# E of the first pair behind the split of x's weighted copy on ACT instead of behind weight splits

## The chip, the core and the metric

The kernel runs on one core of a Trainium2 chip. The core has a matrix engine (PE, with its weight loads PEld), a vector engine (DVE), an activation engine (ACT), a third elementwise engine that here mostly issues DMAs (POOL), and a sequencer for DMA issues (SP). Each engine runs its own instructions in order and waits on semaphores for the others. The metric is the device time of one execution in microseconds.

## The reference: what is computed

One layer of a hybrid encoder, for 256 frames of a new stream and 16 frames of each of 8 running streams, so 384 rows of width 2048, all in float32:

```
u = RMSNorm(x); P = u @ w_in          # columns: pool | z | x,B,C | dt | gates
branch A: trailing-window means of pool columns, per-group linear map, scale
branch B: causal conv (4 taps) + SiLU on x,B,C; Mamba-2 scan over chunks:
  cum   = cumsum(dt * A)
  decay = exp(where(causal, cum[t] - cum[s], -inf))
  y     = einsum(cb[..., None] * decay, x * dt) + C.h * exp(cum)
  h     = h * exp(last) + einsum(B, exp(last - cum), x * dt)
  y += D * x;  RMSNorm(y * SiLU(z))
m = sigmoid(gA) * (A @ w_pool_proj) + sigmoid(gB) * (B @ w_ssd_proj)
x += RMSNorm(m @ w_out);  x += RMSNorm(relu(RMSNorm(x) @ w_up)^2 @ w_down)
```

There are 64 heads of 64 channels in 8 groups with a state of 128. `cb * decay`, for two heads at a time, is what the kernel calls E.

## The kernel before

**Matmuls in three parts.** Every weight block (128 x 1024 float32, 512 KB, eight 128 x 128 tiles) is loaded by SP into a tile `w` and then split in two: ACT makes the rounded high part `wh` (L70) and DVE the rest, `wl = w - wh` (L71). A product is three matmuls per tile: `wh` times the high part of x (L98), `wh` times its low part (L99), `wl` times its high part (L100). A projection `proj` onto 128 columns uses two such blocks (`half` 0 and 1 of 24 matmuls each, 48 in all). `w`, `wh` and `wl` have three buffers each, so a split cannot begin before PE is done with the block three places earlier, and a load not before the split that frees its `w`.

**The stage of the change** is the loop over the eight groups g of branch B. For a group, PE runs ten projections in a row: B and C, four x (`pj_x`), four z (`pj_z`). Between them, chained behind the last matmul (`lump`), stand the small products of the scan. A group has two pairs of x tiles, `D.p[0]` and `D.p[1]`, each of four heads. `xside(S)` makes for a pair x times dt (`xdt`) and x weighted by the decay to the end (`xdw`), and splits `xdw` in a high and a low part: the high part is the ACT instruction on L749, the low part DVE's on L750. `eside(S, q)` makes the half q of the pair's E, two heads: on ACT eight 128 x 128 instructions (L767 an Exp, L769 a Relu, for each head one and three) and two Exp passes over the result (L777, L778), then on DVE one multiplication with the masked `cb` (L779). `t_Y` multiplies E by `xdt` on PE, much later, after the four z projections.

**The functions of ACT need tables.** Where ACT goes from Exp to SiLU or back, an ACT_TABLE_LOAD stands ahead. The taps of the conv end in a SiLU (L606, tile `xs`), and so do the z tiles (L926, tile `zs`).

**What sets the order.** The program is traced once and laid out per engine by a scheduler that may move an instruction ahead of others on its engine unless something holds it. `behind(ins)` is such a hold: what is traced in its block stands after `ins` on `ins`'s engine. `later()` holds behind the last weight split that has been traced:

```
cut[0] = s.activation(h, w, AF.Copy)                             # L70, in wsplit
cut[1] = v.tensor_tensor(l, w, h.bitcast(F32), ALU.subtract)     # L71
with behind(cut[0]), behind(cut[1]):                             # in later()
```

`take` traces the splits of up to three blocks ahead, so when `eside(S, 0)` of group 0 is traced, the last split is that of block z_0_1, the second half of the first z projection. In groups 1 to 7 `eside` of the first pair has no hold (`nullcontext`), before as after. POOL issues the loads of the states (`pload`), SP those of weights and of the running sums `cbc` (`cload`) that `eside` reads.

## Time and profile before

| | |
|---|---|
| median of 3 runs | 2655.93 us (2655.49 to 2656.94) |
| profiled execution | 2658.64 us, its span 2656.9 us |
| PE busy | 2643.5 us, 99% of the span |
| DVE, ACT busy | 1528.7 us (58%), 1173.9 us (44%) |
| granted PE clock, mean | 0.998 of full |
| DMA | 451.48 MB, mean 170 GB/s |

In a timeline a row is start, duration, engine, line, operation and tiles, and in brackets the idle time before it and who ended it. Matmuls overlap in the records, so the pace of PE is read from the distance between two starts, not from a duration. In a table by stretches the columns are the stretch and its length, busy time and instructions of each engine, the granted PE clock, the DMA share and GB/s.

### The profile page before, as it was taken

How to read it: one execution, taken by the hardware profiler on the slowest of the kernel's cores; microseconds unless marked ns; L12 is line 12 of the kernel's file. 1: busy time of each engine (PE TensorE's matmuls, PEld its weight loads, DVE VectorE, ACT ScalarE, POOL GpSimd, SP SyncE). 2: the span in 40 equal slices, each digit the busy share in tenths (PEclk: the TensorE clock that was granted, in tenths of full speed). 3: DMA queues.
4: the chain of work that ended last, by engine and by line, in shares of the span. 5: the costliest groups of instructions: out<-in, count | busy, mean ns of one | idle time of the engine just before them, and what ended most of it. 6: DMA issues, size and time to landing. Idle time of an engine off the chain costs nothing.

```text
span 2656.9 us, 40484 instructions
## 1 busy us (share of the span) xinstructions
PE 2643.5 (99%) x16181; PEld 2543.9 (96%) x16181; DVE 1528.7 (58%) x2152; ACT 1173.9 (44%) x1831; POOL 150.5 (6%) x198
## 2 busy tenths in 40 slices
PE   9999999999999999999999999999999999999998
PEld 9999999999999999999999989999999999999897
DVE  6685335688787888766444436534444444444446
ACT  6443224757566656645333335433333333323233
POOL 0000000011110111020000000000000000000000
PEclk9999999999999999999999999999999999999999
DMA  7444445566666666657544544444443344444433
GB/s 274 149 133 159 147 147 197 178 210 208 221 220 207 206 234 209 228 206 249 177 159 160 182 164 138 141 136 135 135 135 135 135 135 135 135 135 137 135 136 132
DMA packets 147196, 451.48 MB, mean 170 GB/s; under 512 B 18432, under 2 KB 45632, under 8 KB 142016
## 3 DMA queue, kind: packets, MB, share of 16 engines
q1 hardware_dynamic: 134400, 389.90, 44.4%
q0 software_dynamic: 12608, 59.00, 6.0%
q8 instruction: 127, 2.08, 0.3%
q14 instruction: 61, 0.50, 0.1%
HBM read 407.11 MB, written 41.72 MB: 169 GB/s over the span
## 4 chain that ended last, share of the span: by engine, by line
PE 97%; ACT 1%; DVE 1%; issue 1%; DMA 0%; DVEq 0%; POOL 0%; ACTq 0%; POOLq 0%
PE pj_up L98 6%; PE pj_up L100 6%; PE pj_up L99 6%; PE wd L144 6%; PE wd L145 6%; PE wd L143 6%; PE pj_x L98 5%; PE pj_x L100 4%; PE pj_x L99 4%; PE pj_sp L99 3%; PE pj_sp L98 3%; PE pj_sp L100 3%; PE pj_z L100 3%; PE pj_z L98 3%; PE pj_z L99 3%; PE pj_gb L98 2%
## 5 line engine op out<-in xcount | busy, mean ns | idle before, releaser
L98 PE MATMUL pj_up<-x1h,wh_up 128*128 128x384 f32 (+1 forms) x1024 | 334.3, 326 | 0.0
L100 PE MATMUL pj_up<-x1h,wl_up 128*128 128x384 f32 (+1 forms) x1024 | 334.0, 326 | 0.0
L99 PE MATMUL pj_up<-x1l,wh_up 128*128 128x384 f32 (+1 forms) x1024 | 334.0, 326 | 0.0
L71 DVE TENSOR_TENSOR wl_wd<-w_wd,wh_wd 128x1024 fp32r<-128x1024 f32 x126 | 154.4, 1225 | 239.8 <-ACT wh_wd L70 239.8
L144 PE MATMUL wd<-wl_wd,hh 128*128 128x512 f32 x756 | 287.0, 380 | 0.0
L145 PE MATMUL wd<-wh_wd,hl 128*128 128x512 f32 x756 | 287.0, 380 | 0.0
L143 PE MATMUL wd<-wh_wd,hh 128*128 128x512 f32 x756 | 286.9, 380 | 0.0
L70 ACT ACTIVATE wh_wd<-w_wd 128x1024 fp32r<-128x1024 f32 x126 | 133.1, 1057 | 321.5 <-PE wd L145 261.0
L70 ACT ACTIVATE wh_up<-w_up 128x1024 fp32r<-128x1024 f32 x126 | 133.2, 1057 | 292.0 <-PE pj_up L99 231.7
L71 DVE TENSOR_TENSOR wl_up<-w_up,wh_up 128x1024 fp32r<-128x1024 f32 x126 | 154.4, 1225 | 178.0 <-ACT wh_up L70 177.9
L98 PE MATMUL pj_x<-xgh,wh_x 128*128 128x384 f32 x768 | 252.3, 329 | 0.0
L100 PE MATMUL pj_x<-xgh,wl_x 128*128 128x384 f32 x768 | 250.9, 327 | 0.1
L99 PE MATMUL pj_x<-xgl,wh_x 128*128 128x384 f32 x768 | 250.8, 327 | 0.0
L99 PEld LDWEIGHTS pj_up<-x1l,wh_up 128*128 128x128 f32 x1024 | 194.0, 189 | 0.2
L98 PEld LDWEIGHTS pj_up<-x1h,wh_up 128*128 128x128 f32 x1024 | 194.0, 189 | 0.2
L100 PEld LDWEIGHTS pj_up<-x1h,wl_up 128*128 128x128 f32 x1024 | 194.0, 189 | 0.0
L98 PE MATMUL pj_z<-xgh,wh_z 128*128 128x384 f32 x512 | 168.5, 329 | 2.3 <-ACT wh_z L70 2.3
L100 PE MATMUL pj_z<-xgh,wl_z 128*128 128x384 f32 x512 | 168.6, 329 | 0.9 <-DVE wl_z L71 0.9
L99 PE MATMUL pj_z<-xgl,wh_z 128*128 128x384 f32 x512 | 168.3, 329 | 0.0
L99 PE MATMUL pj_sp<-abl,wh_sp 128*128 128x384 f32 x512 | 167.2, 327 | 0.0
L98 PE MATMUL pj_sp<-abh,wh_sp 128*128 128x384 f32 x512 | 167.2, 327 | 0.0
L100 PE MATMUL pj_sp<-abh,wl_sp 128*128 128x384 f32 x512 | 167.2, 327 | 0.0
(334 smaller groups left out, 6135.9 us busy)
## 6 DMA issues: line engine op xcount, KB each, us to landing
w_up<-w_up SPq DMA_DIRECT2D x128, 512.0 KB, 3.5
w_wd<-w_down SPq DMA_DIRECT2D x128, 512.0 KB, 3.4
w_x<-w_in SPq DMA_DIRECT2D x96, 512.0 KB, 4.0
w_z<-w_in SPq DMA_DIRECT2D x64, 512.0 KB, 3.6
w_sp<-w_ssd SPq DMA_DIRECT2D x64, 512.0 KB, 3.5
w_ga<-w_ga SPq DMA_DIRECT2D x32, 512.0 KB, 3.5
w_pp<-w_pp SPq DMA_DIRECT2D x32, 512.0 KB, 3.5
hs<-ssm POOLq DMA_DIRECT2D x16, 1024.0 KB, 7.0
```

Source lines behind the costliest of these rows:

```text
L70: cut[0] = s.activation(h, w, AF.Copy)
L71: cut[1] = v.tensor_tensor(l, w, h.bitcast(F32), ALU.subtract)
L98: te.matmul(out, wh, xh, start=first, stop=False, **how)
L99: te.matmul(out, wh, xl, start=False, stop=False, **how)
L100: return te.matmul(out, wl, xh, start=False, stop=last, **how)
L143: te.matmul(out, mh, vh, start=k == 0, stop=False)
L144: te.matmul(out, mh, vl, start=False, stop=False)
L145: last[0] = te.matmul(out, ml, vh, start=False, stop=k == nk - 1)
```

## The change

`xside` keeps the ACT instruction that makes the high part of `xdw` as `S.split`, and in group 0 both halves of E of the first pair are held behind that instruction, on ACT alone, instead of behind the last weight split on ACT and the last one on DVE.

```
@@ -746,7 +746,7 @@
             S.xhl = pd.tile([P, 2, 2, 3, P], F32R, tag="xhl", name=f"xhl{S.nm}", bufs=1)
-            s.activation(S.xhl[:, 0], S.xdw, AF.Copy)
+            S.split = s.activation(S.xhl[:, 0], S.xdw, AF.Copy)
@@ -915,7 +915,7 @@
-            with nullcontext() if g else later():
+            with nullcontext() if g else behind(S.split):
                 eside(S, 0)
@@ -928,7 +928,7 @@
             pload(D.p[1])
-            with nullcontext() if g else later():
+            with nullcontext() if g else behind(S.split):
                 eside(S, 1)
```

No instruction of PE or POOL changes its place. On SP only the load of the second pair's `cbc_1_1` and that of the weight block z_3_1 change places. On ACT and DVE the change is confined to the z projections of group 0, and two table loads fewer stand there in all (six instead of eight).

The first place is ACT from the split of `xdw` to the split of block z_1_0 (`wh_z_1_0`, first half of the second z projection). A name's first numbers are group, or projection and half, and the last is a buffer. Before, the rows ahead of `wh_z_1_0` are:

```order
L600 ACTIVATE cacc_4641<-cbuf_4125,vec 128x384
L767 ACT_TABLE_LOAD
L767 ACTIVATE E_0_4648<-cbc_0_0_4362,tok 128x128
L769 ACTIVATE E_0_4648<-cbc_0_0_4362,tok 128x128
L606 ACT_TABLE_LOAD
L606 ACTIVATE xs_4646<-cacc_4641,vec 128x384
L769 ACTIVATE E_0_4648<-cbc_0_0_4362,tok 128x128 x2
L777 ACT_TABLE_LOAD
L777 ACTIVATE E_0_4648<-E_0_4648 128x2x128
L778 ACTIVATE E_0_4648<-E_0_4648 128x2x256
L70 ACTIVATE wh_z_1_0_4663<-w_z_1_0_4661 128x1024
```

Now a table load and seven of E's eight first instructions stand between the split of `xdw` and `wh_z_0_1`, and from there on ACT has:

```order
L70 ACTIVATE wh_z_0_1_4608<-w_z_0_1_4606 128x1024
L769 ACTIVATE E_0_4648<-cbc_0_0_4362,tok 128x128
L777 ACTIVATE E_0_4648<-E_0_4648 128x2x128
L778 ACTIVATE E_0_4648<-E_0_4648 128x2x256
L767 ACTIVATE E_0_4648<-cbc_0_1_4364,tok 128x128
L769 ACTIVATE E_0_4648<-cbc_0_1_4364,tok 128x128 x3
L606 ACT_TABLE_LOAD
L606 ACTIVATE xs_4573<-cacc_4568,vec 128x384
L70 ACTIVATE wh_z_1_0_4663<-w_z_1_0_4661 128x1024
L593 COPY cbuf_4125<-cbuf_4125 128x15x3
L594 COPY cstate<-cbuf_4125 128x27
L600 ACTIVATE cacc_4641<-cbuf_4125,vec 128x384
```

So `wh_z_1_0` has moved ahead of the last x tile's taps and of the SiLU of `xs_4646`; it stood behind both.

The second place is ACT up to the next block, `wh_z_1_1`. Before, it follows `wh_z_1_0` almost at once, and E's second half comes behind it:

```order
L70 ACTIVATE wh_z_1_0_4663<-w_z_1_0_4661 128x1024
L592 COPY cbuf_4123<-cstate 128x8x3
L592 COPY cbuf_4125<-cstate 128x8x3
L70 ACTIVATE wh_z_1_1_4693<-w_z_1_1_4691 128x1024
L767 ACTIVATE E_0_4648<-cbc_0_1_4364,tok 128x128
L769 ACTIVATE E_0_4648<-cbc_0_1_4364,tok 128x128 x3
```

Now the rest of E's second half and the last taps stand ahead of it (the rows that follow the fence of the first place):

```order
L767 ACT_TABLE_LOAD
L767 ACTIVATE E_0_4648<-cbc_0_1_4364,tok 128x128
L769 ACTIVATE E_0_4648<-cbc_0_1_4364,tok 128x128 x3
L606 ACT_TABLE_LOAD
L606 ACTIVATE xs_4646<-cacc_4641,vec 128x384
L777 ACT_TABLE_LOAD
L777 ACTIVATE E_0_4648<-E_0_4648 128x2x128
L778 ACTIVATE E_0_4648<-E_0_4648 128x2x256
L592 COPY cbuf_4123<-cstate 128x8x3
L592 COPY cbuf_4125<-cstate 128x8x3
L70 ACTIVATE wh_z_1_1_4693<-w_z_1_1_4691 128x1024
```

So `wh_z_1_1` now comes after the whole of E, where it came after half of it.

The third place is DVE at the same time; here is one piece of the difference:

```order
 L71 TENSOR_TENSOR wl_z_0_1_4609<-w_z_0_1_4606,wh_z_0_1_4608 128x1024
+L779 TENSOR_TENSOR E_0_4648<-E_0_4648,cbm_4566 128x1024
 L586 TENSOR_TENSOR cbuf_4125<-pj_x_4575,rstd 128x12x16 x2
+L71 TENSOR_TENSOR wl_z_1_0_4664<-w_z_1_0_4661,wh_z_1_0_4663 128x1024
 L602 TENSOR_SCALAR cacc_4641<-cbuf_4125,vec,cacc_4641 128x384 x3
 L779 TENSOR_TENSOR E_0_4648<-E_0_4648,cbm_4566 128x1024
-L71 TENSOR_TENSOR wl_z_1_0_4664<-w_z_1_0_4661,wh_z_1_0_4663 128x1024
 L71 TENSOR_TENSOR wl_z_1_1_4694<-w_z_1_1_4691,wh_z_1_1_4693 128x1024
```

The multiplication of E's first half now stands ahead of the eviction of the last x tile (L586), `wl_z_1_0` ahead of that tile's taps, and the multiplication of the second half directly ahead of `wl_z_1_1`.

More of the change, by code (lines that the diff above doesn't have):

```diff
@@ L748, in xside @@
             S.xhl = pd.tile([P, 2, 2, 3, P], F32R, tag="xhl", name=f"xhl{S.nm}", bufs=1)
-            s.activation(S.xhl[:, 0], S.xdw, AF.Copy)
+            S.split = s.activation(S.xhl[:, 0], S.xdw, AF.Copy)
             v.tensor_tensor(S.xhl[:, 1], S.xdw, S.xhl[:, 0].bitcast(F32), ALU.subtract)
@@ L917, in build @@
             D.xs.append(conv(u0 + 5, g * 4 + 3, "xs", 6))
-            with nullcontext() if g else later():
+            with nullcontext() if g else behind(S.split):
                 eside(S, 0)
@@ L930, in build @@
             pload(D.p[1])
-            with nullcontext() if g else later():
+            with nullcontext() if g else behind(S.split):
                 eside(S, 1)
```

## The prediction

> **What bounds the kernel now.** I read the busy shares first, then the chain that ended last, then what PE itself waited for.

> ```profile
> PE 2643.5 (99%) x16181; PEld 2543.9 (96%) x16181; DVE 1528.7 (58%) x2152; ACT 1173.9 (44%) x1831; POOL 150.5 (6%) x198
> ...
> PE 97%; ACT 1%; DVE 1%; issue 1%; DMA 0%; DVEq 0%; POOL 0%; ACTq 0%; POOLq 0%
> ```

> PE is the bound. Work that another engine saves is worth nothing unless PE was waiting for it. These are all of PE's waits in the whole span (engine, line, releaser: us in total, times, longest):

> ```profile
> PE pj_z L98 <- ACT wh_z L70: 2.3, 1, 2.3
> PE warm_o L231 <- DVE warm L227: 1.2, 1, 1.2
> PE pj_z L100 <- DVE wl_z L71: 0.9, 1, 0.9
> PE pj_p L307 <- ACT xgh L267: 0.4, 1, 0.4
> ```

> Two of the four fall in the z projections, once each, so in one group. They stand at one place, at the start of the second z projection of group 0 (PE's timeline; the first row is the first matmul of the first z projection):

> ```profile
> 470.30 0.33 PE L98 MATMUL pj_z<-xgh,wh_z 128*128 128x384 f32 x1
> ...
> 477.94 0.33 PE L100 MATMUL pj_z<-xgh,wl_z 128*128 128x384 f32 x1
> 480.58 0.43 PE L98 MATMUL pj_z<-xgh,wh_z 128*128 128x384 f32 x1 [2.32 <-ACT wh_z L70]
> 480.85 0.33 PE L99 MATMUL pj_z<-xgl,wh_z 128*128 128x384 f32 x1
> 482.03 0.69 PE L100 MATMUL pj_z<-xgh,wl_z 128*128 128x384 f32 x1 [0.85 <-DVE wl_z L71]
> 482.51 0.53 PE L98 MATMUL pj_z<-xgh,wh_z 128*128 128x384 f32 x1
> ...
> 487.94 0.33 PE L100 MATMUL pj_z<-xgh,wl_z 128*128 128x384 f32 x1
> ```

> The 48 matmuls of the first projection start from 470.30 to 477.94, so 7.64 / 47 = 0.1625 us apart. The second should begin at 478.10 and begins at 480.58. But after the wait the matmuls are 0.32 us apart, up to 487.94. The table by stretches says why; its stretches of 3.41 us end where the pace changes, and the number after the POOL column is the granted clock:

> ```profile
> 477.64:481.05 3.41, 1.09 (x6) 0.62 (x5) 1.43 (x2) 3.40 (x7) 0.00 (x0) 1.00 0.01 4
> 481.05:484.46 3.41, 2.56 (x9) 2.43 (x9) 2.53 (x3) 3.40 (x9) 0.00 (x0) 0.51 0.38 126
> 484.46:487.87 3.41, 3.41 (x12) 3.41 (x11) 0.00 (x0) 3.37 (x6) 0.00 (x0) 0.50 1.01 347
> 487.87:491.28 3.41, 3.41 (x22) 3.41 (x22) 3.14 (x3) 2.14 (x3) 0.00 (x0) 0.99 0.18 66
> ```

> PE was busy for 1.09 of 3.41 us, and then had half its clock for two stretches of that length. So the wait costs about twice its own size.

> **What the place costs.** The matmul at 487.94 is the 21st of its projection (three rows to 482.03, the fourth at 482.51, then 17 steps). Without a wait it would start at 478.10 + 20 x 0.1625 = 481.35. The loss is 6.59 us: 2.48 for the late high part, 1.02 for the late low part (482.03 instead of 480.85 + 0.16), 17 x 0.1625 = 2.67 (5.43 measured, 2.76 at full pace) for the half clock, and 0.42 for the two long steps after the waits.

> **The change, part by part.** Why the high part was late stands in ACT's timeline, which has no idle time from 466.44 on:

> ```profile
> 462.13 0.84 ACT L749 ACTIVATE xhl<-xdw 128x768 fp32r<-128x768 f32 x1 [0.16 <-DVE xdw L735]
> 466.44 1.06 ACT L70 ACTIVATE wh_z<-w_z 128x1024 fp32r<-128x1024 f32 x1 [3.46 <-PE pj_x L99]
> 467.51 1.28 ACT L767 ACT_TABLE_LOAD   x1
> 468.81 0.40 ACT L767 ACTIVATE E<-cbc,tok 128x128 f32<-128x128 f32 x1
> 469.11 0.97 ACT L769 ACTIVATE E<-cbc,tok 128x128 f32<-128x128 f32 x3
> 470.11 1.28 ACT L606 ACT_TABLE_LOAD   x1
> 471.40 0.61 ACT L606 ACTIVATE xs<-cacc,vec 128x384 f32<-128x384 f32 x1
> 471.92 0.22 ACT L593 COPY cbuf<-cbuf 128x45 f32<-128x45 f32 x1
> ...
> 472.83 1.28 ACT L767 ACT_TABLE_LOAD   x1
> ...
> 476.14 0.62 ACT L606 ACTIVATE xs<-cacc,vec 128x384 f32<-128x384 f32 x1
> ...
> 478.65 0.42 ACT L777 ACTIVATE E<-E 128x256 f32<-128x256 f32 x1
> 478.97 0.61 ACT L778 ACTIVATE E<-E 128x512 f32<-128x512 f32 x1
> 479.49 1.04 ACT L70 ACTIVATE wh_z<-w_z 128x1024 fp32r<-128x1024 f32 x1
> 480.44 0.31 ACT L592 COPY cbuf<-cstate 128x24 f32<-128x24 f32 x2
> 480.65 1.05 ACT L70 ACTIVATE wh_z<-w_z 128x1024 fp32r<-128x1024 f32 x1
> ```

> ACT stands idle for 3.46 us after the split of xdw (462.97), since wh_z_0_1 has to wait for PE to free a buffer, and E may not start before it. After it, 12 us of E, taps and five table loads hold wh_z_1_0 back to 479.49. Now E goes into the idle time. I use distances between starts: a table load 1.29, four first instructions of E up to a table load 1.30 (468.81 to 470.11), one without a load behind it 0.30, a SiLU 0.52, L777 0.32, L778 0.52, a weight split 0.95.

> *First step.* Load at 463.0, seven instructions of E from 464.3 to 466.4. That just fills the gap: wh_z_0_1 stays at 466.44, PE's release. PE needs it at 474.2, so even a miss is covered. The next pieces: E 467.39, L777 467.69, L778 468.01, four of E 468.53, load 469.83, SiLU 471.12, and **wh_z_1_0 at 471.64**, 7.85 us earlier than before. Its buffer is free when the last x projection ends at 470.3, and its load was issued with the first z blocks. On DVE the multiplication of E (1.14) comes after wl_z_0_1 and delays the eviction of the last x tile from 470.50 to 471.6; PE asks for that bank again at 478.10, so this is free. Then wl_z_1_0 ends at about 473.9, 4 us before PE needs it. Both waits and the half clock go: **-6.59 us**.

> *Second step: what is late next.* Ahead of wh_z_1_1 now stand copies and tap 0.91 (471.92 to 472.83), load 1.30, four of E 1.30, load 1.29, SiLU 0.62, load 1.29, L777, L778 0.84 and L592 0.21. From 472.59 that gives 480.35 for wh_z_1_1 and 481.4 for its end. PE needs it at 482.00. Its low part is tighter. On DVE:

> ```profile
> 472.85 1.93 DVE L602 SCALAR_TENSOR_TENSOR cacc<-cbuf,vec,cacc 128x384 f32<-128x384 f32 x3 [1.73 <-ACT cacc L600]
> 479.62 1.23 DVE L779 TENSOR_TENSOR E<-E,cbm 128x1024 f32<-128x1024 f32 x1 [4.84 <-ACT E L778]
> 480.76 2.35 DVE L71 TENSOR_TENSOR wl_z<-w_z,wh_z 128x1024 fp32r<-128x1024 f32 x2
> ```

> L602 takes 1.93, and the SiLU behind it finds its taps done (475.7 against 477.4). The multiplication of E's second half must wait for L778 (ends 480.25), holds DVE to 481.4, and wl_z_1_1 ends at 482.65. PE's third matmul of that half would start at 482.33. A wait of this kind, and what it does to the clock, stands elsewhere in the trace:

> ```profile
> 439.73 0.33 PE L99 MATMUL pj_x<-xgl,wh_x 128*128 128x384 f32 x1
> 440.14 0.43 PE L100 MATMUL pj_x<-xgh,wl_x 128*128 128x384 f32 x1
> 440.41 0.33 PE L98 MATMUL pj_x<-xgh,wh_x 128*128 128x384 f32 x1
> ```

> There the low part cost 0.25 and the long step 0.11, and the next pace was full. I take 0.33 + 0.11: **+0.4 us**; bounds 0 (my chain is 0.33 pessimistic) and 2.0 (it slips by as much as the old wait's 2.3). Behind it come the eviction of z_0 and wl_z_2_0, which with a split at 1.23 are done by about 484.5; PE needs that block at 486.3. wh_z_2_1, behind a table load and the SiLU of z_0, comes near 484.2 and is needed at 490.2.

> *Loads.* SP's order up to wh_z_2_1 is unchanged: the block z_1_1 is issued behind the scatter of the states at 473.39.

> ```profile
> 473.39 0.84 SPq L63 DMA_DIRECT2D w_z<-w_in  x2
> ...
> DMA to landing us min/median/max: 3.4/3.7/5.1
> ```

> Landed by 478.5, it is 1.9 us ahead of 480.35. Since wl_z_1_0 frees its w 8 us earlier, a third load joins these two; 1.57 MB at the 347 GB/s of the busiest stretch above is 4.5 us, so even shared they are there by 478.4. The second pair's cbc_1_1 changes places with w_z_3_1, neither of which is near its use. The two table loads fewer and the earlier E are worth nothing: E is read by PE after the four z projections.

> *Sum.* -6.59 + 0.4 = -6.2 us. All later waits of PE are nil, so the rest shifts as it is. The profiled execution would take 2658.64 - 6.2 = 2652.4 us. It is 2.71 above the median; against the median 2655.93 the sum gives **2649.7 us**.

> [...] A table load starts 0.01 us after the end of the last instruction, which it lets run out (0.40 instead of 0.30), and the next starts 1.29 to 1.30 after it; a switch costs 1.4 us here. [...]

> **The rivals.** *The timed runs do not pay the half clock.* The clock changes at 481.05, 484.46 and 487.87, on a beat of 3.41 us with no instruction at it. If the beat lies otherwise in another run, the 3.17 us of waiting may be split between two stretches, and neither is empty enough to trip it. Then before pays 2.67 less, which is nearly the 2.71 by which the profiled execution is above the median. That speaks for it. Against it: the three runs differ by only 1.45 us, and 3.2 of 3.8 us idle fill most of any stretch. Gain 6.59 - 2.67 - 0.4 = 3.5: 2652.4 us, or about 2651.1 if half of the slow time is paid. [...]

> *The new wait grows.* If wh_z_1_1 or its load is 1 to 2 us later than worked out, PE waits that much at 482.0, without the half clock: 2650.7 to 2651.7 us.

> [...]

> **How the numbers follow.** The full gain has 0.62, the missing half clock 0.28, the grown wait 0.06, slower 0.04, of which 0.03 beyond 0.2%. About 0.2%, 5.3 us, is what a measurement of this kernel can tell from no change, so the border lies at 2650.6: the full gain is beyond it by 0.9 only, the first two rivals are within it. That makes faster 0.62, within 0.35, slower 0.03. The range goes from the full 6.59 less 0.7 for the spread of the runs (2648.6) to the missing half clock with the same 0.7 and 0.3 of further wait (2653.4).

> **What would show it.** In the profile after, PE's wait for wh_z is gone and the granted clock is 1.00 between 470 and 500; wh_z_1_0 starts near 471.6 and wh_z_1_1 near 480.4; ACT is busy from 463 on; the only new wait is about 0.3 us for wl_z near 482.3; the z projections take 7.8 us each. A wait for wh_z at 482, or a clock of 0.50 behind it, would prove the second step wrong; a gain of 3 us with a clean trace would prove the first rival.

## The result and the profile after

| | before | after |
|---|---|---|
| median | 2657.18 us (2655.46 to 2658.9, 20 runs) | 2651.89 us (2650.89 to 2652.5, 20 runs) |
| ratio, 95% interval | | 0.998 (0.9973 to 0.9987) |
| profiled execution, span | 2656.9 us | 2649.6 us |

The kernel became 5.29 us faster by the medians, 0.199%, a hair below the 0.2% that the prediction took as its border; the interval of the ratio excludes no change, and in microseconds it runs from about 3.5 to 7.2. The median of before over 20 runs is 1.25 us above that of its first three.

PE's waits in the profile after, all of them (engine, line, releaser: us in total, times, longest):

```profile
PE warm_o L231 <- DVE warm L227: 1.2, 1, 1.2
PE pj_p L98 <- ACT wh_e L291: 0.6, 1, 0.6
PE pj_p L307 <- ACT xgh L267: 0.4, 1, 0.4
PE pj_p L307 <- DVE xgl L269: 0.2, 1, 0.2
PE pj_z L100 <- DVE wl_z L71: 0.2, 1, 0.2
```

The wait of 2.3 us for a high part is gone, that of 0.9 for a low part is down to 0.2. The rows of pj_p lie in the first 10 us of the kernel, ahead of the change; more on them below. PE's timeline shows it at the half of the second z projection. The first row is the first z matmul, the last row the first of the small products behind the four z projections:

```profile
469.12 0.33 PE L98 MATMUL pj_z<-xgh,wh_z 128*128 128x384 f32 x1
...
480.99 0.33 PE L99 MATMUL pj_z<-xgl,wh_z 128*128 128x384 f32 x1
481.51 0.43 PE L100 MATMUL pj_z<-xgh,wl_z 128*128 128x384 f32 x1 [0.20 <-DVE wl_z L71]
481.78 0.33 PE L98 MATMUL pj_z<-xgh,wh_z 128*128 128x384 f32 x1
...
500.79 0.83 PE L692 MATMUL py<-xhl,Bhl 128*128 128x256 f32 x6
```

The step from 480.99 to 481.51 is 0.52 instead of 0.16, the next 0.27: together 0.47 us lost. The clock did not fall (table by stretches, the number after the POOL column):

```profile
477.50:482.50 5.00, 4.80 (x30) 4.50 (x29) 3.44 (x4) 4.96 (x9) 0.00 (x0) 1.00 0.33 129
482.50:487.50 5.00, 5.00 (x33) 5.00 (x32) 3.47 (x4) 2.91 (x4) 0.00 (x0) 1.00 0.79 250
```

The four z projections are 192 matmuls of 0.1625, 31.2 us. From the first of them to the small products it takes 31.67 us now (500.79 - 469.12). In the same profile of before as in the prediction, the row that ends this stretch is

```profile
508.09 0.83 PE L692 MATMUL py<-xhl,Bhl 128*128 128x256 f32 x6
```

so it took 508.09 - 470.30 = 37.79 us there. The place gave 6.12 us between the two profiles. The spans differ by 7.3, since the z projections also begin 1.18 us earlier. That part has nothing to do with the change, for up to there PE has the same instructions in the same order. 0.36 of it is the wait at 440.14 that the prediction shows, which this profile of after does not have. The other 0.82 is what is left, after 16 us, of the pace of the very first matmuls (before first, then after):

```profile
5.44 1.17 PE L307 MATMUL pj_p<-xgh,wh_e 128*128 128x384 f32 x3
6.40 1.17 PE L307 MATMUL pj_p<-xgl,wh_e 128*128 128x384 f32 x3
```

```profile
5.21 0.65 PE L307 MATMUL pj_p<-xgh,wh_e 128*128 128x384 f32 x3
5.70 0.65 PE L307 MATMUL pj_p<-xgl,wh_e 128*128 128x384 f32 x3
```

Three matmuls take 0.96 us there and 0.49 here: before runs at half pace up to about 10 us, after is at full pace from its first float32 matmul at 4.3 us on. That costs before up to 2.5 us (the last row at L307 starts at 10.64 there and at 8.14 here), and most of it comes back at the first weights, where the earlier PE has a wait (0.6 us in the list above) and longer steps and the later one does not. Behind the small products the two are alike: 2656.9 - 508.09 and 2649.6 - 500.79 are both 2148.81.

ACT, in after:

```profile
461.82 1.28 ACT L767 ACT_TABLE_LOAD   x1
463.11 0.40 ACT L767 ACTIVATE E<-cbc,tok 128x128 f32<-128x128 f32 x1
...
465.26 1.06 ACT L70 ACTIVATE wh_z<-w_z 128x1024 fp32r<-128x1024 f32 x1
...
470.44 1.04 ACT L70 ACTIVATE wh_z<-w_z 128x1024 fp32r<-128x1024 f32 x1
...
476.80 1.28 ACT L777 ACT_TABLE_LOAD   x1
478.09 0.42 ACT L777 ACTIVATE E<-E 128x256 f32<-128x256 f32 x1
478.42 0.61 ACT L778 ACTIVATE E<-E 128x512 f32<-128x512 f32 x1
478.94 0.31 ACT L592 COPY cbuf<-cstate 128x24 f32<-128x24 f32 x2
479.15 2.01 ACT L70 ACTIVATE wh_z<-w_z 128x1024 fp32r<-128x1024 f32 x2
```

Add 1.18 to compare with before: wh_z_1_0 starts at 471.62, wh_z_1_1 at 480.33.

### The profile page after: what moved, and what is told of

Read it like the earlier page. It is cut to its first block, busy times and chain, and to the rows that moved or that the text cites. A ratio compares the mean times of both kernels' runs of the same rounds, so it can differ in the third digit from the quotient of the medians.

```text
span 2649.6 us, 40482 instructions
## 1 busy us (share of the span) xinstructions
PE 2638.2 (100%) x16181; PEld 2537.1 (96%) x16181; DVE 1528.0 (58%) x2152; ACT 1171.5 (44%) x1829; POOL 150.5 (6%) x198
## 4 chain that ended last, share of the span: by engine, by line
PE 98%; ACT 1%; DVE 1%; DMA 0%; issue 0%; SPq 0%; DVEq 0%; ACTq 0%
PE pj_up L98 6%; PE pj_up L100 6%; PE pj_up L99 6%; PE wd L145 6%; PE wd L144 6%; PE wd L143 6%; PE pj_x L98 5%; PE pj_x L100 5%; PE pj_x L99 5%; PE pj_sp L99 3%; PE pj_sp L100 3%; PE pj_sp L98 3%; PE pj_z L100 3%; PE pj_z L99 3%; PE pj_z L98 3%; PE pj_gb L98 2%
## 5 line engine op out<-in xcount | busy, mean ns | idle before, releaser
L98 PE MATMUL pj_up<-x1h,wh_up 128*128 128x384 f32 (+1 forms) x1024 | 333.7, 326 | 0.0
L99 PE MATMUL pj_up<-x1l,wh_up 128*128 128x384 f32 (+1 forms) x1024 | 333.4, 326 | 0.0
L100 PE MATMUL pj_up<-x1h,wl_up 128*128 128x384 f32 (+1 forms) x1024 | 333.4, 326 | 0.0
L71 DVE TENSOR_TENSOR wl_wd<-w_wd,wh_wd 128x1024 fp32r<-128x1024 f32 x126 | 154.3, 1225 | 239.9 <-ACT wh_wd L70 239.9
L70 ACT ACTIVATE wh_wd<-w_wd 128x1024 fp32r<-128x1024 f32 x126 | 133.1, 1057 | 321.5 <-PE wd L145 261.0
L70 ACT ACTIVATE wh_up<-w_up 128x1024 fp32r<-128x1024 f32 x126 | 133.1, 1056 | 291.7 <-PE pj_up L99 231.8
L71 DVE TENSOR_TENSOR wl_up<-w_up,wh_up 128x1024 fp32r<-128x1024 f32 x126 | 154.3, 1225 | 177.8 <-ACT wh_up L70 177.7
L98 PE MATMUL pj_x<-xgh,wh_x 128*128 128x384 f32 x768 | 251.9, 328 | 0.0
L99 PE MATMUL pj_x<-xgl,wh_x 128*128 128x384 f32 x768 | 250.4, 326 | 0.0
L100 PE MATMUL pj_x<-xgh,wl_x 128*128 128x384 f32 x768 | 250.4, 326 | 0.0
L99 PEld LDWEIGHTS pj_up<-x1l,wh_up 128*128 128x128 f32 x1024 | 193.6, 189 | 0.2
L98 PEld LDWEIGHTS pj_up<-x1h,wh_up 128*128 128x128 f32 x1024 | 193.6, 189 | 0.2
L100 PEld LDWEIGHTS pj_up<-x1h,wl_up 128*128 128x128 f32 x1024 | 193.6, 189 | 0.0
L100 PE MATMUL pj_z<-xgh,wl_z 128*128 128x384 f32 x512 | 167.0, 326 | 0.2 <-DVE wl_z L71 0.2
L98 PE MATMUL pj_z<-xgh,wh_z 128*128 128x384 f32 x512 | 166.9, 326 | 0.0
L99 PE MATMUL pj_z<-xgl,wh_z 128*128 128x384 f32 x512 | 166.9, 326 | 0.0
L98 PE MATMUL pj_sp<-abh,wh_sp 128*128 128x384 f32 x512 | 166.9, 326 | 0.0
L99 PE MATMUL pj_sp<-abl,wh_sp 128*128 128x384 f32 x512 | 166.9, 326 | 0.0
L100 PE MATMUL pj_sp<-abh,wl_sp 128*128 128x384 f32 x512 | 166.9, 326 | 0.0
```

Of the source, the lines that this page charges most:

```text
L98: te.matmul(out, wh, xh, start=first, stop=False, **how)
L99: te.matmul(out, wh, xl, start=False, stop=False, **how)
L100: return te.matmul(out, wl, xh, start=False, stop=last, **how)
```

## The experiments

Six more kernels were run, and before was profiled twice more. For each, the time from the first z matmul to the small products (the place) is read from its profile as above; the medians stand beside the medians of before on the same chip.

| kernel | first z matmul | small products | place | median | before there |
|---|---|---|---|---|---|
| before | 470.30 | 508.09 | 37.79 | 2657.18 | |
| look_1 (before again) | 468.78 | 505.18 | 36.40 | 2655.72 (1 run) | 2656.97 |
| look_2 (before again) | 468.05 | 505.91 | 37.86 | 2656.45 (1 run) | 2656.97 |
| fill14 | 469.28 | 504.92 | 35.64 | 2655.9 | 2657.28 |
| fill7 | 468.90 | 504.54 | 35.64 | 2656.0 | 2657.28 |
| first_half | 468.71 | 502.66 | 33.95 | 2653.22 | 2657.28 |
| second_half | 469.08 | 500.94 | 31.86 | 2651.61 | 2656.97 |
| after | 469.12 | 500.79 | 31.67 | 2651.89 | 2657.18 |
| mul_later | 468.65 | 500.33 | 31.68 | 2651.71 | 2657.28 |
| exp_later | 468.73 | 499.93 | 31.20 | 2651.41 | 2656.97 |

**Is the half clock the wait's doing?** Matmuls whose result nobody reads were put into PE's idle time; they add work to the computation and change nothing else of it. fill14 has 14 of them, as below, and fill7 has 7.

```
+            def fill(n):
+                o = sstile("fill")
+                for _ in range(n):
+                    i = te.matmul(pairs(o[:, :T]), onesr, woven(xg[0][0]), start=True, stop=True)
+                return i
+            if g == 0:
+                lump(lambda: fill(14))
             zproj(1)
```

> The kernel before, with 14 matmuls (128x384, result unused) put on PE between the first and the second z projection of group 0, where PE stands idle for 2.3 us. The wait stays, only PE's idleness goes. Theory: the half clock comes from the empty stretch on PE, so it goes: granted clock 1.00 from 478 to 490, the second z projection's 4th to 21st matmul 0.16 us apart, and from the first matmul of the first z projection to the first of the third 22.19 - 2.67 - 0.2 = 19.3 us. In the timed runs it is worth less than 2.67, since the place gave 6.12 us between the two profiles but the medians differ by 5.29: about 1.8 us faster than before. Rival (the clock falls for another reason, such as the DMA load or the tables on ACT): 22.2 us and no gain.

> As the kernel with 14 matmuls, with 7: PE is busy for the first 1.14 us of the wait and idle for the other 1.2, then once more for 0.85. Theory, if any stretch that is over half empty halves the clock: about 2 us of 3.41 are still empty when a stretch falls on both waits, so it halves in some executions and not in others; the median lies between before and the kernel with 14, 0.5 to 1.5 us faster than before, and the runs are as far apart as those of before (3.4 us). If the clock falls only after one unbroken empty piece of about 2 us, it is as the kernel with 14: about 1.8 us faster, runs within 1.6 us.

PE's timeline with 14:

```profile
477.08 2.44 PE L936 MATMUL fill<-xgh,onesr 128*128 128x384 f32 x14
479.57 0.43 PE L98 MATMUL pj_z<-xgh,wh_z 128*128 128x384 f32 x1
481.01 0.43 PE L100 MATMUL pj_z<-xgh,wl_z 128*128 128x384 f32 x1 [0.85 <-DVE wl_z L71]
...
488.59 0.33 PE L98 MATMUL pj_z<-xgh,wh_z 128*128 128x384 f32 x1
488.76 0.33 PE L99 MATMUL pj_z<-xgl,wh_z 128*128 128x384 f32 x1
489.54 0.43 PE L100 MATMUL pj_z<-xgh,wl_z 128*128 128x384 f32 x1 [0.46 <-DVE wl_z L71]
```

and its clock:

```profile
480.00:485.00 5.00, 4.15 (x25) 3.99 (x25) 2.56 (x3) 4.97 (x12) 0.00 (x0) 1.00 0.56 169
485.00:490.00 5.00, 4.54 (x29) 4.25 (x28) 2.87 (x3) 4.97 (x7) 0.00 (x0) 1.00 0.51 198
```

The clock stays at 1.00 though the splits are as late as before (wh_z_1_0 starts 9.19 us behind the first z matmul in both profiles), and the third z projection starts 19.31 us after the first (488.59 - 469.28), as expected. So the empty stretch on PE did it. But then something shows that the profile of before had hidden: PE, now earlier, waits in the third projection too, for the low part of z_2_0, which in before stands behind the second half of E. That wait (0.46, with its steps 0.73) was covered by the slow matmuls. So the half clock costs 37.79 - 35.64 = 2.15 us net: the 2.67 of the prediction, some 0.2 of the long step that it counted apart, less the 0.73. By the medians fill14 gains 1.4 us where 1.8 was expected, with an interval that just includes none (0.9985 to 1.0003); in its profile it also took 0.5 us more from the place to the last z matmul on L98 (1133.8 - 504.92 = 628.9, against 1129.2 - 500.79 = 628.4 in after), the cause of which stays open.

With 7 matmuls (idle 1.19 and 0.85 us) the place is the same 35.64: in the execution that was profiled these two waits did not halve the clock (the matmuls behind them, from 480.90 to 488.38, stay 0.16 us apart), though one stretch of the beat, counted from the change of pace at the start of that profile, was 1.3 us empty:

```profile
478.74:482.16 3.42, 2.11 (x11) 1.82 (x12) 3.42 (x4) 3.42 (x11) 0.00 (x0) 1.00 0.09 19
```

The runs lie within 2.5 us, between the 3.4 and the 1.6 of the two expectations, and the median is 1.3 us below that of before.

**How often is it paid?** Before was profiled twice more, unchanged.

> The kernel before once more, one profile. Theory: the beat of the clock lies differently in each execution. In one in which the half clock is paid, from the first z matmul to the small products it takes 37.8 us; in one in which it is not, it takes 35.64 us as with the fill, with a wait of 0.46 us for a low part in the third z projection that the half clock covers otherwise. Changes of pace at the start and at the place lie a multiple of 3.41 us apart. Rival: the half clock is paid in every execution alike, 37.8 us, and the spread of before's runs (3.8 us) has another cause.

> The same as the first look, in another execution: 37.8 us with a stretch at half clock of 6.8 us or 3.4 us, or 35.64 us without; the first z matmul starts anywhere from 468.6 to 470.3, by how long the start ran at half pace.

The first late matmul in the first look, in PE's timeline, and then in the second:

```profile
479.07 0.43 PE L98 MATMUL pj_z<-xgh,wh_z 128*128 128x384 f32 x1 [2.32 <-ACT wh_z L70]
```

```profile
478.34 0.43 PE L98 MATMUL pj_z<-xgh,wh_z 128*128 128x384 f32 x1 [2.32 <-ACT wh_z L70]
```

The stretches of the first look, cut where the pace changes:

```profile
476.75:480.16 3.41, 0.59 (x2) 0.30 (x2) 2.06 (x2) 3.40 (x8) 0.00 (x0) 1.00 0.00 0
480.16:483.57 3.41, 3.06 (x10) 3.06 (x11) 1.90 (x3) 3.39 (x10) 0.00 (x0) 0.50 0.55 163
483.57:486.98 3.41, 3.41 (x22) 3.41 (x22) 0.35 (x1) 3.38 (x6) 0.00 (x0) 1.00 0.95 352
```

and of the second:

```profile
475.60:479.01 3.41, 1.01 (x5) 0.41 (x3) 1.64 (x2) 3.40 (x7) 0.00 (x0) 1.00 0.00 0
479.01:482.42 3.41, 2.63 (x8) 2.64 (x9) 2.32 (x3) 3.41 (x9) 0.00 (x0) 0.50 0.46 158
482.42:485.84 3.42, 3.42 (x12) 3.42 (x12) 0.00 (x0) 3.38 (x7) 0.00 (x0) 0.50 0.93 308
```

The first look pays one slow stretch, the second two, like the profile in the prediction. The beat of 3.41 us is the same in all three, its place against the instructions is not: the last empty stretch ends 1.09 us after the first late matmul in one (479.07 to 480.16) and 0.67 in the other (478.34 to 479.01). In the first PE is busy for 3.06 of the next 3.41 us, and the clock comes back behind them; in the second, with 2.63, it does not. The change of pace at the start comes at 5.7 us in the first look and at 4.5 in the second, some 474.5 us ahead of the fall in both, which is 139 beats of 3.41 (474.5 / 139 = 3.414), as was expected. So the place costs 36.4 or 37.8 us, and after gains 4.7 or 6.1 on it. The median gain of 5.29 lies between. The look expected 37.8 or 35.64; 36.4 is a third case. The first z matmul of the second look, at 468.05, lies below the 468.6 that was expected.

How often the half clock is paid can be read from the mean granted clock, which is on record for each of 53 runs of before: it is 0.998 in 48 of them and 0.999 in five, which took 2654.8 to 2655.7 us. In all 63 runs of after, second_half, mul_later, exp_later and fill14 it is 0.999. In the profiles of before and after the clock is at half for the last 4.9 and 3.6 us of the span, behind PE's last matmul, which by itself leaves a mean of 0.9991 and 0.9993; a mean that rounds to 0.998 takes some 8 us at half clock (0.0015 x 2655 / 0.5). My estimate from these numbers is that such a run had a slow stretch besides, as the three profiles of before have, each with a mean of 0.998. At least 48 of the 53 thus paid one or two stretches. The five may have paid one or none, and one is not told from two by this number.

**Which half of the change does it?** One hold was changed at a time.

```
-            with nullcontext() if g else behind(S.split):
+            with nullcontext() if g else later():
                 eside(S, 1)        # first_half; eside(S, 0) in second_half
```

> The kernel before with only the hold of E's first half changed; the second half stays behind the weight splits. Theory: both blocks of the second z projection are then split early (no wait there), but the whole second half of E with three table loads stands ahead of the split z_2_0: by the rows of after it starts near 485.9 on the profile's clock of before, where PE asks for it at 485.9, and its low part comes 2.2 us too late. So the wait moves one projection on, with 1.0 us for the high and 1.2 us for the low part, without or with part of the half clock: 6.6 - 2.2 = 4.4 us faster than before at best, 1.5 to 2 with the half clock. Rival (the first half alone was in the way): as after, 5 to 6 us faster.

> The kernel before with only the hold of E's second half changed; the first half stays behind the split z_0_1. ACT then fills its gap with seven instructions of the second half, and the first half and two Exp passes with three table loads stand ahead of the split z_1_0. Theory, from the rows of before: it starts near 477.7 instead of 479.5 on before's clock, where PE asks at 478.1; its low part, begun when the high part is done, is 0.5 us late and z_1_1 then is not. Loss at the place 0.5 to 0.7 us, no half clock: 37.8 - 5.9 = 31.9 us from the first z matmul to the small products, 2652.0 us. Rival (only the first half matters, as the gap belongs to it): both waits stay, 2656 us or more.

With the first half alone, the wait moves on to the third z projection:

```profile
485.83 0.43 PE L98 MATMUL pj_z<-xgh,wh_z 128*128 128x384 f32 x1 [1.35 <-ACT wh_z L70]
487.28 0.43 PE L100 MATMUL pj_z<-xgh,wl_z 128*128 128x384 f32 x1 [0.85 <-DVE wl_z L71]
```

Its place is 33.95, 2.75 more than the bare matmuls, in this profile without the half clock. The median is 4.1 us faster than before, against 4.4 expected at best; eight of its eleven runs lie from 2652.4 to 2653.4 and three from 2654.4 to 2655.8. Two of these three, 2654.43 and 2655.82, have a mean clock of 0.998 and so a slow stretch by the reckoning above; all others have 0.999. The same holds for the slowest run of fill7, 2657.16. In the profile of first_half PE was busy for 2.06 us of the emptiest stretch of the beat, and the clock did not fall behind it (1.00 from 486.8 to 490.2):

```profile
482.77:486.18 3.41, 2.06 (x13) 1.71 (x11) 1.31 (x2) 3.41 (x8) 0.00 (x0) 1.00 0.21 83
```

With the second half alone, PE waits only 0.39 us, for the low part of z_1_0, and the runs are as fast as those of after:

```profile
477.76 0.43 PE L100 MATMUL pj_z<-xgh,wl_z 128*128 128x384 f32 x1 [0.39 <-DVE wl_z L71]
```

Seven of E's instructions and the table load fit into ACT's gap either way. What differs is where the other half is left, and that is worth 33.95 - 31.86 = 2.1 us. In second_half the first half stands between wh_z_0_1 and wh_z_1_0, where ACT has time for it: wh_z_1_0 starts at 475.40 and PE asks for it at 476.88. In first_half the second half stands behind wh_z_1_1 with three table loads, and wh_z_2_0 starts at 484.74, where PE asks at 484.3. ACT in second_half, then in first_half:

```profile
475.40 1.04 ACT L70 ACTIVATE wh_z<-w_z 128x1024 fp32r<-128x1024 f32 x1
```

```profile
484.74 2.93 ACT L70 ACTIVATE wh_z<-w_z 128x1024 fp32r<-128x1024 f32 x3
```

The hold of the second half alone thus gives the whole gain that was measured (2651.61 against 2651.89); that of the first half adds 0.19 us at the place, which the medians cannot tell.

**What is left of the wait?** Two kernels hold more of the second half behind the splits of z_1_1: only the multiplication (mul_later), or the two Exp passes as well (exp_later).

```
-            v.tensor_tensor(Eq, Eq, S.D.cbm.unsqueeze(1).to_broadcast([P, 2, 512]), ALU.mult)
+            with behind(hold):                                # mul_later
+                v.tensor_tensor(Eq, Eq, S.D.cbm.unsqueeze(1).to_broadcast([P, 2, 512]), ALU.mult)
...
-                eside(S, 1)
+                eside(S, 1, None if g else cut[1])            # mul_later
...
+            with hold():                                      # exp_later
+                s.activation(Eq[:, :, :P], Eq[:, :, :P], AF.Exp, scale=-1.0)
+                s.activation(Eq[:, :, TP:], Eq[:, :, TP:], AF.Exp, scale=-1.0)
+                v.tensor_tensor(Eq, Eq, S.D.cbm.unsqueeze(1).to_broadcast([P, 2, 512]), ALU.mult)
...
+                eside(S, 1, nullcontext if g else later)      # exp_later
```

> The kernel after, with the multiplication of E's second half held on DVE behind the split wl_z_1_1 instead of ahead of it. Theory: the low part then ends 1.1 us earlier, the last wait of PE at the second z projection goes, and from the first z projection to the third PE takes 15.6 instead of 16.07 us: 0.47 us faster than after, 5.3 + 0.5 = 5.8 us faster than before. Rival: the multiplication now delays the eviction of z_0 and the next split, and the 0.4 us appear again at the third projection: no gain against after.

> The kernel after with the two Exp passes and the multiplication of E's second half held behind the splits of z_1_1, on ACT and DVE. The run with the multiplication alone held there left PE's 0.22 us wait as it was, since the low part begins when the high part ends on ACT. Theory: ACT's chain is what is late, and without the table load (1.28) and the two passes (0.84) wh_z_1_1 starts 2.1 us earlier, its low part ends 2 us before PE needs it, and z_2_0 follows with 0.8 us to spare. No wait of PE in the z projections; from the first z matmul to the small products 31.2 instead of 31.67 us; 0.4 to 0.5 us faster than after, 2651.3 us. Rival: the passes and table loads behind z_1_1 make z_2_0 late instead: 31.7 us or more.

mul_later changed nothing: 31.68 us. The 0.47 us that were expected did not come, and the wait did not move to the third projection either, as its rival had it. ACT, then DVE, then PE in its timeline:

```profile
478.69 2.00 ACT L70 ACTIVATE wh_z<-w_z 128x1024 fp32r<-128x1024 f32 x2
```

```profile
479.77 1.23 DVE L71 TENSOR_TENSOR wl_z<-w_z,wh_z 128x1024 fp32r<-128x1024 f32 x1 [5.66 <-ACT wh_z L70]
```

```profile
481.06 0.43 PE L100 MATMUL pj_z<-xgh,wl_z 128*128 128x384 f32 x1 [0.22 <-DVE wl_z L71]
```

DVE is free now, and the split begins no earlier: the high part on ACT ends at that very moment (478.69 + 1.05 = 479.74, the low part starts at 479.77). In after both were ready within 0.1 us of each other (ACT's split ends at 480.20, DVE's multiplication at 480.28), and only the later one can be seen. exp_later takes the table load and the passes out of ACT's way: the high part of z_1_1 starts at 476.52, PE has no wait in the z projections, and the place is 31.20 us, the matmuls alone.

```profile
476.30 0.31 ACT L592 COPY cbuf<-cstate 128x24 f32<-128x24 f32 x2
476.52 1.05 ACT L70 ACTIVATE wh_z<-w_z 128x1024 fp32r<-128x1024 f32 x1
```

Its median, 2651.41 us, is 0.48 below that of after, which is what the place says; the two were not run in one comparison and their runs overlap. Its place is the shortest of all; that it beats after or second_half in time is not shown.

## Why the prediction was right or wrong, point by point

- *PE bound, one place with a wait and a half clock behind it, 6.59 us in that profile:* right. With the matmuls at 31.2 us, the place stands at 37.79, which is 6.59 more.
- *First step:* right. wh_z_1_0 was put at 471.64 and came at 471.62 on before's clock. The load and seven instructions filled the gap, wh_z_0_1 started at 465.26 (466.44), and the late eviction of the last x tile cost nothing: PE has no wait for it.
- *Second step:* the size was right, 0.44 expected and 0.47 measured, wh_z_1_1 at 480.35 expected and 480.33 measured. The reason given, that E's multiplication holds up the low part on DVE, was only half of it. My own two numbers for ACT and DVE both said 481.4, and I named one. mul_later and exp_later show that ACT's end decides as well. The splits behind it came when they were expected: wl_z_2_0 was done at 484.23 on before's clock (484.5), and wh_z_2_1 started at 484.08 (484.2). So the rival of a grown wait did not come.
- *Sum:* 6.2 expected, 6.12 between the two profiles, but 5.29 between the medians. The term that was mis-sized is the half clock, taken as 2.67 us in every execution. It is 2.15 net with two slow stretches (they cover 0.73 of waiting in the third z projection, of which the profile of before shows nothing), and in the first look only 36.40 - 35.64 = 0.76 net with one. The profiles show this; the medians alone do not, since 6.2 lies within their interval. That the sum comes so near to 6.12 is no test of this term: the profile of before is the one the sum was read from, and it paid two slow stretches.
- *First rival, no half clock in the timed runs:* its premise, a beat that lies otherwise in another run, was right: in the three profiles of before the clock fell 0.47, 1.09 and 0.67 us behind the first late matmul. Its conclusion was not: by the estimate from the mean clock at least 48 of 53 runs of before paid a slow stretch. Its price was not either: without one the gain would be 35.64 - 31.67 = 4.0 by fill14's place, not 3.5. What I held to speak for it, the 2.71 us by which the profiled execution was above the median, had in good part another cause: the three profiles of before begin their z projections at 468.05, 468.78 and 470.30, so the one in the prediction lost 1.5 to 2.2 us at the very start.
- *Slower:* did not come. In after the instruction behind a table load starts 1.29 us after the load began (461.82 to 463.11), as in before (470.11 to 471.40).
- *The time:* 2649.7 against 2651.89. Of the 2.2 us, 1.25 is the median of before, which three runs put too low, and 0.9 is the gain that was put too high, for which the half clock is the cause that the profiles offer. The forecast of a gain beyond 0.2% missed by almost nothing, 0.199%.

## What to carry to other kernels

Look for the gap in the engine that prepares operands (here 3.46 us on ACT before a split that must wait for a buffer) and move into it what stands ahead of a later split. What does not fit should be left ahead of a split that has time to spare: here that choice was worth 2.1 us. Price a wait of the matmul engine with the slow matmuls behind it (here 2.15 us net with two slow stretches, 0.76 with one), and expect that removing it uncovers waits which these had covered (here 0.46 us in the third z projection). Where two engines become ready at the same moment, moving one of them alone gains nothing (here 31.68 us in mul_later against 31.67 in after).

## What the runs showed of the hardware

```profile
3.22:6.64 3.42, 3.05 (x8) 1.97 (x7) 2.09 (x5) 1.95 (x4) 0.00 (x0) 1.00 0.93 315
```

```profile
0.67:4.09 3.42, 2.74 (x6) 0.74 (x6) 0.50 (x2) 1.75 (x2) 0.20 (x1) 1.00 0.63 193
```

- The start of the kernel varies too: in the ten profiles in the table the first z matmul stands anywhere from 468.05 to 470.30 us, with the same work ahead of it, and the first row of three matmuls takes 0.48 us in first_half, 0.49 in after and 0.96 in before and mul_later. Before, in which the half pace lasts to 10.1 us, has the latest z matmul, but the pace of the first matmuls does not settle it: mul_later has its z matmul at 468.65, and after at 469.12. This is a spread of more than two microseconds that no change to the kernel's middle explains.
